# Hybrid decoder layer, one core: gate and up of the two FFNs with tokens stationary in blocks of 512 columns each, two of eight feature pairs by Strassen's products

## The chip, the cores and the metric

The kernel runs on one core of a Trainium2 chip. The metric is the device time of one execution in microseconds, lower is better. TensorE is called PE here, VectorE DVE, ScalarE ACT, GpSimd POOL, and SyncE SP (it issues the loads).

## The reference, cut to what matters

One layer for 256 tokens with 2048 features, in float32: an FFN, a mixing stage with two attentions, and a second FFN.

```python
def swiglu(x, w_gate, w_up, w_down):
    return (jax.nn.silu(x @ w_gate) * (x @ w_up)) @ w_down
...
f = swiglu(rmsnorm(x, ffn1_pre_g[l]), ffn1_w_gate[l], ffn1_w_up[l], ffn1_w_down[l])
x = x + FFN_RES_SCALE * rmsnorm(f, ffn1_post_g[l])
h = rmsnorm(x, mix_pre_g[l])
...
x = x + rmsnorm(o @ w_out[l], mix_post_g[l])
f = swiglu(rmsnorm(x, ffn2_pre_g[l]), ffn2_w_gate[l], ffn2_w_up[l], ffn2_w_down[l])
x = x + FFN_RES_SCALE * rmsnorm(f, ffn2_post_g[l])
```

Each FFN has 5632 hidden features: `w_gate` and `w_up` are 2048 x 5632, `w_down` is 5632 x 2048. A feature tile is 128 features, so the inputs have 16 tiles (8 pairs) and the hidden layer has 44 (22 pairs). A token tile is 128 tokens; there are two, t=0 and t=1.

## The kernel before

**Float32 in two halves.** Every operand of a large product is split into a high part `hi` and a rest `lo`, and a product is made of hi·hi, hi·lo and lo·hi. The class `Weights` loads weights in float32 into one of three buffers (`raw`, 1 MB each), SP issuing the loads in a fixed order. It then splits them into parts of up to 1024 columns: ACT casts the high part (`whi`, L133), DVE subtracts it from the original to give the rest (`wlo`, L138). There are four buffers for parts, and `get` asks for parts three ahead of the one that PE takes. So the cast of a part waits until PE has finished with the part four before it.

**Gate and up.** `gate_up(fp)` makes 256 gate features and 256 up features (the number `fp` runs from 0 to 21). Weights are stationary, x is the moving operand: for each input tile and each of two output tiles there is one product of `whi` with [hi x, lo x] side by side, 512 columns (L493), and one of `wlo` with hi x, 256 columns (L502). A part holds four input tiles, so it is 8 products of each kind. x itself is not yet scaled by the token's norm; the results are, by a row `pre.R` (L735, L743). The output has features on the partitions, as the down product needs it as its stationary operand; `put_h` splits it, and for the pairs that go by Strassen's products forms their sums first (`sum_h`).

**Down.** The class `Down` (L804) works with tokens stationary: h is the stationary operand and the weights move, 512 columns at a time. A pair of feature tiles times two chunks of 512 columns is a 2 x 2 block product. Plain, it takes 24 products into four accumulators, called 2, 3, 4 and X. By Strassen's scheme in Winograd's form (`BY_SUMS`, 4 of 11 pairs) it takes 7 block products, 21 in all, into seven accumulators 1 to 7; DVE forms the sums of the weights in place in the raw buffer (`add_sums`, L101 to L107), which makes a pair four parts instead of two. PSUM has eight banks of 512 columns. `middle` joins the seven accumulators, `finish` adds the last four.

**Order.** The hidden layer is done in two halves of 11 pairs: gate and up of a half, then its down products for two column ranges `u`. Steps of other engines are queued by `later(n, ...)` and taken up, one entry a part, by `step()`. Inside the handovers from one stage to the next (`handover`, `take_over`, `start`) the order is written out by hand; elsewhere a scheduler orders each engine's instructions and hands out PSUM banks and the 28 SBUF slots as they come free. POOL is used in the handovers and in the rotary part of one attention. The residual x stays in SBUF (`xn`) all the time.

## Time and profile before

| | |
|---|---|
| median of 3 runs | 1886.82 us (1886.21 to 1886.95) |
| the profiled execution | 1886.46 us, of which span 1884.4 us |
| granted PE clock, mean | 0.994 |
| busy | PE 98%, DVE 71%, ACT 51%, POOL 5% of the span |
| DMA | 188 GB/s, the core's engines 55% busy with the weights |

The span runs from the first to the last instruction; 2.06 us lie around it. Busy shares are averages over the stages. A matmul's own duration contains its latency, so what it costs is read from the spacing of starts, not from its duration.

### The profile page before, as it was taken

The numbers are of one execution on the slowest core, as the hardware profiler recorded it, in microseconds if no ns is written. First come the engines' busy times: TensorE is split into PE (matmuls) and PEld (weight loads), VectorE is DVE, ScalarE is ACT, GpSimd is POOL, SyncE is SP. The second block draws the span as 40 slices with busy tenths as digits, with TensorE's granted clock in tenths as the row PEclk, the third lists the DMA queues.
The fourth block names the chain that finished last, engine by engine and source line by source line (L and its number), as shares of the span: only waits on it lengthen the run. The fifth ranks groups of instructions, "written<-read, shape, count | busy, mean of one in ns | idle before, by whom it ended". The sixth has DMA issues, their size and how long they took to land.

```text
span 1884.4 us, 25317 instructions
## 1 busy us (share of the span) xinstructions
PE 1853.7 (98%) x9802; PEld 1595.8 (85%) x9802; DVE 1342.1 (71%) x1998; ACT 965.5 (51%) x1411; POOL 103.0 (5%) x92
## 2 busy tenths in 40 slices
PE   9999999999999998999999999999999999999997
PEld 8888888888888887788888887888888888888885
DVE  6666688766666998666786557766678766666897
ACT  6444455544444555645545446544455544444553
POOL 0000000000000002000352103000000000000001
PEclk9999999999999999999999999999999999999998
DMA  8555555665655554554445555555555665555453
GB/s 270 179 196 184 190 190 201 223 201 180 197 183 191 191 194 161 184 186 161 157 157 183 181 172 172 186 194 187 187 192 202 223 200 180 194 187 187 172 200 134
DMA packets 260120, 353.73 MB, mean 188 GB/s; under 512 B 5856, under 2 KB 219040, under 8 KB 259616
## 3 DMA queue, kind: packets, MB, share of 16 engines
q1 hardware_dynamic: 259552, 351.30, 55.1%
q8 instruction: 77, 1.26, 0.3%
q0 software_dynamic: 272, 0.75, 0.1%
q14 instruction: 43, 0.35, 0.1%
q10 hardware_dynamic: 176, 0.07, 0.0%
HBM read 350.00 MB, written 2.10 MB: 187 GB/s over the span
## 4 chain that ended last, share of the span: by engine, by line
PE 94%; DVE 4%; ACT 1%; issue 1%; POOL 0%; DMA 0%; DVEq 0%; ACTq 0%; POOLq 0%
PE p L493 34%; PE d L822 20%; PE p L502 18%; PE pq L493 5%; PE pw L512 4%; PE pv L512 4%; PE d_X L822 4%; PE pq L502 3%; DVE wlo L138 1%; DVE xn L673 1%; PE po L1020 0%; PE xt_f L456 0%; ACT sqd L365 0%; PE p L497 0%; ACT whi L133 0%
## 5 line engine op out<-in xcount | busy, mean ns | idle before, releaser
L138 DVE TENSOR_TENSOR wlo<-raw,whi 128x1024 fp32r<-128x1024 f32 (+1 forms) x717 | 859.3, 1209 | 487.5 <-ACT whi L133 482.3
L133 ACT CAST whi<-raw 128x1024 fp32r<-128x1024 f32 (+1 forms) x721 | 736.9, 1030 | 768.5 <-PE p L493 374.7
L493 PE MATMUL p<-xg_f,whi 128*128 128x512 f32 x2784 | 698.9, 392 | 0.0
L493 PEld LDWEIGHTS p<-xg_f,whi 128*128 128x128 f32 x2784 | 500.4, 189 | 89.2
L502 PEld LDWEIGHTS p<-xg_f,wlo 128*128 128x128 f32 x2816 | 384.8, 190 | 27.7
L502 PE MATMUL p<-xg_f,wlo 128*128 128x256 f32 x2816 | 394.0, 282 | 0.0
L822 PE MATMUL d<-whi,h 128*128 128x512 f32 x672 | 207.5, 389 | 0.0
L822 PEld LDWEIGHTS d<-whi,h 128*128 128x128 f32 x672 | 126.1, 188 | 26.2
L493 PE MATMUL pq<-xg_mix,whi 128*128 128x512 f32 x512 | 131.8, 399 | 0.0
L822 PE MATMUL d<-wlo,h 128*128 128x512 f32 x336 | 114.7, 390 | 0.0
L493 PEld LDWEIGHTS pq<-xg_mix,whi 128*128 128x128 f32 x512 | 92.2, 189 | 16.9
L512 PE MATMUL pv<-whi,xg_mix 128*128 128x512 f32 x256 | 85.4, 405 | 1.7 <-ACT xg_mix L422 1.7
L822 PE MATMUL d_X<-whi,h 128*128 128x512 f32 x224 | 85.5, 389 | 0.0
L652 ACT COPY right<-p 128x256 f32<-128x256 f32 x176 | 60.1, 370 | 45.5 <-PE p L493 40.9
L512 PE MATMUL pw<-whi,om 128*128 128x512 f32 x256 | 75.2, 391 | 0.0
L822 PEld LDWEIGHTS d<-wlo,h 128*128 128x128 f32 x336 | 62.9, 188 | 13.6 <-DVE wlo L138 0.6
L502 PEld LDWEIGHTS pq<-xg_mix,wlo 128*128 128x128 f32 x512 | 69.8, 190 | 5.3
L822 PE MATMUL d<-whi,hi 128*128 128x512 f32 x224 | 72.2, 390 | 1.3 <-ACT whi L133 1.3
L822 PE MATMUL d<-wlo,hi 128*128 128x512 f32 x224 | 71.8, 390 | 0.0
L822 PE MATMUL d<-whi,ho 128*128 128x512 f32 x224 | 71.6, 389 | 0.0
L502 PE MATMUL pq<-xg_mix,wlo 128*128 128x256 f32 x512 | 71.3, 282 | 0.0
L138 POOL TENSOR_TENSOR wlo<-raw,whi 128x512 fp32r<-128x512 f32 (+1 forms) x10 | 17.8, 1786 | 824.2 <-DVE rs_post_f L349 729.7
(198 smaller groups left out, 1486.5 us busy)
## 6 DMA issues: line engine op xcount, KB each, us to landing
raw<-in_ffn_w_down_dram SPq DMA_DIRECT2D x86, 1024.0 KB, 5.0
raw<-in_ffn_w_gate_dram SPq DMA_DIRECT2D x84, 1024.0 KB, 5.0
raw<-in_ffn_w_up_dram SPq DMA_DIRECT2D x84, 1024.0 KB, 5.0
raw<-in_w_in_dram SPq DMA_DIRECT2D x48, 1024.0 KB, 5.2
raw<-in_w_out_dram SPq DMA_DIRECT2D x16, 1024.0 KB, 4.9
raw<-in_ffn_w_up_dram SPq DMA_DIRECT2D x8, 512.0 KB, 3.5
raw<-in_ffn_w_gate_dram SPq DMA_DIRECT2D x7, 512.0 KB, 3.8
xn<-in_x_dram SPq DMA_DIRECT2D x8, 256.0 KB, 6.0
```

Of the source, the lines that this page charges most:

```text
L133: self.nc.scalar.copy(hi, raw)
L138: eng.tensor_sub(lo[:, k0:k1], raw[:, k0:k1], hi[:, k0:k1].bitcast(F32))
L493: nc.tensor.matmul(p, wh, x, start=k == 0, stop=False)
L502: nc.tensor.matmul(p[:, :T], lo[:, j, f * P:(f + 1) * P], xs(k)[:, 0, :], start=False, stop=k == KD - 1)
L512: nc.tensor.matmul(ps[c], y, w[:, j, c * CH:(c + 1) * CH], start=first and n == 0, stop=last and n == 2)
L652: nc.scalar.copy(t, ps[:, T:])
L673: nc.vector.scalar_tensor_tensor(x, f, self.z[t], x, op0=ALU.mult, op1=ALU.add)
L822: nc.tensor.matmul(self.ps[x], y, w, start=m == 1, stop=m == self.n[x])
```

## The change

Only `fp` 0 and 1 of each FFN (the first 256 + 256 features each time, which stand in the handover) are still made the old way. From then on, gate and up are made in ten blocks of 512 gate and 512 up columns (`gate_up_block`) by a class `Block` that is the old `Down` made general: x is the stationary operand, the weights move, the two chunks of a 2 x 2 block product are 512 gate and 512 up columns, and two of the eight pairs of input tiles (`X_SUMS`, pairs 1 and 4) go by Strassen's products. Five blocks belong to the first half of the hidden layer, which now has 12 pairs, and five to the second, which has 10; the down products are by sums for 4 pairs of the first half and 3 of the second.

Since the results now have tokens on the partitions, x must be scaled before the products (`scale_x`, on ACT, in place in `xn`), turned and split once more (`put_x`, 32 PE transposes in each FFN, in the last three steps of `fp` 1), and the product h of each block must be turned back into features on partitions (`turn_h`, 8 transposes a block, after the first pair of the next block or of the down product). Accumulators of gate and up are joined, passed through silu and multiplied in `xn`, which serves as scratch. So the residual is kept in DRAM: in FFN 1 it is read again from the input, in FFN 2 it is written out after the handover; both times POOL issues eight loads of 256 KB during the second half's down products. The loads of gate and up become two of 512 KB for each pair instead of one of 1 MB. Gains of rows and the attention's masks move to SBUF slots, of which there are 30 now.

```diff
-BY_SUMS = (0, 2, 4, 6)
-KP = KF // 4
+X_SUMS = (1, 4)
+
+
+FIRST, BLOCKS = 1, (6, 11)
+HALVES = (
+    ((0, 2, 1, 4, 3, 6, 5, 8, 7, 9, 10, 11), (2, 4, 6, 8), ()),
+    ((13, 12, 15, 14, 17, 16, 18), (12, 14, 16), (19, 20, 21)),
+)
+H_SUMS = HALVES[0][1] + HALVES[1][1]
...
-    slots = Slots(ctx.enter_context(tc.tile_pool(name="slots", bufs=1)), 28)
+    slots = Slots(ctx.enter_context(tc.tile_pool(name="slots", bufs=1)), 30)
...
-        for fp in range(KF // 2):
+        for fp in range(2 * FIRST):
...
+        for half in range(2):
+            for u in range(BLOCKS[half - 1] if half else FIRST, BLOCKS[half]):
+                plan["block", n, u] = [
+                    (q, W.add_sums((wg, wu), 2 * q, u * CH) if q in X_SUMS else W.add((wg, wu), 2 * q, 2, u * CH, 2 * CH))
+                    for q in range(KD // 2)
+                ]
+            plan_down(n, half, wd)
...
+                for c in range(NC):
+                    for t in range(NT):
+                        sl = slice(c * CH, (c + 1) * CH)
+                        nc.gpsimd.dma_start(kept[:, t, sl], xn[:, t, sl])
...
+        def sums_of(r, name):
+
+            a21 = r[:, 7]
+            nc.vector.tensor_add(r[:, S1], a21, r[:, A22])
+            nc.vector.tensor_sub(r[:, S3], r[:, A11], a21)
+            nc.vector.tensor_sub(r[:, S2], r[:, S1], r[:, A11])
+            nc.vector.tensor_sub(r[:, S4], r[:, A12], r[:, S2])
+            hi, lo = (slots.take([P, 7, P], F32R, f"{name}{m}") for m in "hl")
+            nc.scalar.copy(hi, r[:, :7])
+            nc.vector.tensor_sub(lo, r[:, :7], hi.bitcast(F32))
+            return hi, lo
...
+        def scale_x(c):
+            for t in range(NT):
+                x = xn[:, t, c * CH:(c + 1) * CH]
+                nc.scalar.activation(x, x, AF.Copy, scale=pre.z[t])
+
+        def put_x(q):
+            ps = bank(f"xt{n}{q}")
+            for j in range(2):
+                for t in range(NT):
+                    m = 2 * j + t
+                    k = 2 * q + j
+                    nc.tensor.transpose(ps[:, m * P:(m + 1) * P], xn[:, t, k * P:(k + 1) * P], ident)
+            name = f"x{n}_{q}"
+            gains = [pre.gains[:, 2 * q + j:2 * q + j + 1] for j in range(2)]
+            if q in X_SUMS:
+                r = slots.take([P, 8, P], F32, f"r{name}")
+                p4 = ps.rearrange("p (m c) -> p m c", c=P)
+                nc.scalar.activation(r[:, 0::7], p4[:, :2], AF.Copy, scale=gains[0])
+                nc.scalar.activation(r[:, 1:3], p4[:, 2:], AF.Copy, scale=gains[1])
+                xx[q] = sums_of(r, name)
+                slots.give(f"r{name}")
+            else:
+                xx[q] = slots.take([P, 2, 2, T], F32R, name)
+                for j in range(2):
+                    for f in split_rows(xx[q][:, j], ps[:, j * T:(j + 1) * T], gains[j]):
+                        f()
...
+                banks(0), banks(1)
+                for c in range(NC):
+                    later(c, lambda c=c: scale_x(c))
+                if n == 1:
+                    later(5, lambda: turn_gains(G, graw, G_END))
+                for q in range(KD // 2):
+                    later(5 + q // 3, lambda q=q: put_x(q))
...
-        class Down:
-
-
-            def __init__(self, half, u):
-                self.half, self.c = half, (2 * u, 2 * u + 1)
+        class Block:
+
+
+            def __init__(self, name, pairs, xs, sums, more=0):
+                self.name, self.pairs, self.xs, self.sums = name, pairs, xs, sums
                 self.ps, self.done = {}, {}
-                self.pairs = plan["down", n, half, u]
-                sums = len(BY_SUMS)
-                self.n = {x: 3 * sums for x in "1234567"}
-                self.n["X"] = 0
-                for x in "234X":
-                    self.n[x] += 6 * (KP - sums)
...
+                by_sums = len([p for p, _ in pairs if p in sums])
+                plain = len(pairs) + more - by_sums
+                self.n = {x: 3 * by_sums * (x != "X") + 6 * plain * (x in "234X") for x in "1234567X"}
...
+
+                def first():
+                    nc.scalar.copy(a, self.ps["1"])
+                    nc.vector.tensor_add(b, self.ps["6"], a)
+                    nc.vector.tensor_sub(c, b, self.ps["5"])
+
+                def second():
+                    nc.vector.tensor_add(d, self.ps["7"], c)
+                    nc.vector.tensor_add(b, self.ps["7"], b)
...
+        def gate_up_block(u):
+
+            tg = [xn[:, 0, m * CH:(m + 1) * CH] for m in range(NC)]
+            blk = Block(f"b{n}{u}", plan["block", n, u], xx, X_SUMS)
+            blk.run(waiting, blk.joins(*(tg[m] for m in (0, 2, 1, 3))), lambda p: None)
+            for c, t in ((1, 0), (0, 0), (0, 1), (1, 1)):
+                blk.join(tg[2 * t + c], c, t)
+            for t in range(NT):
+                g, h = tg[2 * t], tg[2 * t + 1]
+                nc.scalar.activation(g, g, AF.Silu)
+                later(t, lambda g=g, h=h: nc.vector.tensor_mul(h, h, g))
+            waiting.append(lambda: turn_h(u, tg))
+
+        def turn_h(u, tg):
+
+            for m in range(2):
+                p = 2 * u + m
+                name = f"h{n}_{p}"
+                ps = bank(f"ht{n}{p}")
+                p4 = ps.rearrange("p (m c) -> p m c", c=P)
+                for j in range(2):
+                    for t in range(NT):
+                        k = 2 * m + j
+                        nc.tensor.transpose(p4[:, 2 * j + t], tg[2 * t + 1][:, k * P:(k + 1) * P], ident)
+                if p in H_SUMS:
+                    r = xn[:, 1, m * 8 * P:(m + 1) * 8 * P].rearrange("p (m c) -> p m c", c=P)
+                    nc.scalar.copy(r[:, 0::7], p4[:, :2])
+                    nc.scalar.copy(r[:, 1:3], p4[:, 2:])
+                    later(m, lambda p=p, r=r, name=name: hx.__setitem__(p, sums_of(r, name)))
+                else:
+                    hx[p] = slots.take([P, 2, 2, T], F32R, name)
+                    v = ps.rearrange("p (j t) -> p j t", j=2)
+                    nc.scalar.copy(hx[p][:, :, 0], v)
+                    nc.vector.tensor_sub(hx[p][:, :, 1], v, hx[p][:, :, 0].bitcast(F32))
...
+        if n == 1:
+            kept = xv
+        else:
+            kept = tc.dram_tile([P, NT, D], F32, name="kept")
+        for fp in range(2 * FIRST):
+            gate_up(fp)
+        slots.give(*pre.names)
         for half in range(2):
-            for fp in range(half * KP, (half + 1) * KP):
-                gate_up(fp)
+            for u in range(BLOCKS[half - 1] if half else FIRST, BLOCKS[half]):
+                gate_up_block(u)
             if half == 0:
-                post = Post(f"f{n}", row_gain(row_name), half=True)
+                post = Post(f"f{n}", half=True)
             else:
-                slots.give(*pre.names)
+                for q, x in xx.items():
+                    give(x, f"x{n}_{q}")
                 more = [slots.take([P, 2, CH], F32, f"more{n}{m}") for m in range(2)]
+                post.rows = RowGain(row_name)
+                for c in range(NC):
+                    for t in range(NT):
+                        sl = slice(c * CH, (c + 1) * CH)
+                        later(8 + c, lambda t=t, sl=sl: nc.gpsimd.dma_start(xn[:, t, sl], kept[:, t, sl]))
             for u in range(2):
                 d = Down(half, u)
-                d.run()
+                d.go()
                 if (half, u) != (1, 1):
                     for c, t in ((1, 0), (0, 0), (0, 1), (1, 1)):
                         d.finish(c, t)
         d.tail(end_of(post))
-        slots.give(*(f"more{n}{m}" for m in range(2)), *(f"h{n}_{KF // 2 - 3 + m}" for m in range(3)))```

What moves on the engines, at three places. **First, PE in gate and up.** Before, a part looks like this (`p_2_0` and `p_2_1` are the accumulators of two gate tiles, `xg_f` is x turned, `whi` and `wlo` are a part of the weights; of each kind there are eight rows in turn):

```order
L493 MATMUL p_2_0_781<-xg_f_102,whi_725 128x512
L493 MATMUL p_2_1_782<-xg_f_102,whi_725 128x512
...
L493 MATMUL p_2_0_781<-xg_f_103,whi_725 128x512
...
L502 MATMUL p_2_0_781<-xg_f_102,wlo_726 128x256
L502 MATMUL p_2_1_782<-xg_f_102,wlo_726 128x256
...
L502 MATMUL p_2_0_781<-xg_f_103,wlo_726 128x256
```

Now, at the end of a block's first pair (`x_0`) and in its second (`x_1h`, `x_1l`, by sums), with `b_1` to `b_7` and `b_X` the accumulators and `ht` the banks in which the block before is turned:

```order
L872 MATMUL b_4_1471<-whi_1411,x_0_646 128x512
L872 MATMUL b_X<-whi_1411,x_0_646 128x512
L952 MATMUL ht_1497<-ident,xn 128x128
L952 MATMUL ht_1504<-ident,xn 128x128
L872 MATMUL b_1_1519<-whi_1430,x_1h 128x512
...
L872 MATMUL b_2_1463<-whi_1454,x_1l 128x512
L952 MATMUL ht_1497<-ident,xn 128x128 x3
L952 MATMUL ht_1504<-ident,xn 128x128 x3
L872 MATMUL b_5_1545<-whi_1480,x_1h 128x512
...
L872 MATMUL b_7_1547<-whi_1480,x_1h 128x512
...
L872 MATMUL b_6_1558<-whi_1512,x_1h 128x512
```

All products are 512 wide, and eight transposes of the block before stand between them in two groups, the second group after nine products of the second pair; `b_7` and `b_6` come last, in the banks of `ht`.

**Second, DVE between two blocks.** Before, from one `fp` to the next, DVE had splits with steps of 256 columns between them:

```order
L138 TENSOR_TENSOR wlo_848<-raw_829,whi_847 128x1024
L138 TENSOR_TENSOR wlo_870<-raw_829,whi_869 128x1024
L654 TENSOR_TENSOR u<-p_2_0_781,right 128x256
L654 TENSOR_TENSOR g<-p_2_1_667,right 128x256
L743 TENSOR_TENSOR u<-u,R_f_480 128x256
L735 TENSOR_TENSOR g<-g,R_f_480 128x256
L716 TENSOR_TENSOR hr_2_922<-u,g 128x2x128
```

Now the last joins of a block (L924), the sums of the next block's second pair (L104 to L110), its splits (L142) and the product of gate and up (L939, once for each token tile) follow each other:

```order
L142 TENSOR_TENSOR wlo_1431<-raw_1415,whi_1430 128x1024
L924 TENSOR_TENSOR xn<-b_3_1123,xn 128x512
L104 TENSOR_TENSOR raw_1415<-raw_1415 128x512
...
L924 TENSOR_TENSOR xn<-b_4_1129,xn 128x512
L924 TENSOR_TENSOR xn<-b_X,xn 128x512
L142 TENSOR_TENSOR wlo_1455<-raw_1415,whi_1454 128x512
L109 TENSOR_TENSOR raw_1415<-raw_1415 128x512
L939 TENSOR_TENSOR xn<-xn 128x512
L110 TENSOR_TENSOR raw_1415<-raw_1415 128x512
L142 TENSOR_TENSOR wlo_1481<-raw_1415,whi_1480 128x1024
L939 TENSOR_TENSOR xn<-xn 128x512
L142 TENSOR_TENSOR wlo_1513<-raw_1415,whi_1512 128x1024
```

There are ten instructions from the first split to the first L939 (two of them, a join and a sum, are under the dots), and three more to the second; each group of transposes needs one of the L939.

**Third, PE in `fp` 1**, where nothing but products of the first kind stood before:

```order
L525 MATMUL p_1_1_448<-xg_f_103,wlo_515 128x256
L337 MATMUL gp<-ident,graw 128x48
L807 MATMUL xt_641<-ident,xn 128x128 x4
L807 MATMUL xt_651<-ident,xn 128x128 x4
L807 MATMUL xt_667<-ident,xn 128x128 x4
L516 MATMUL p_1_0_447<-xg_f_104,whi_547 128x512
...
L807 MATMUL xt_700<-ident,xn 128x128 x4
L807 MATMUL xt_710<-ident,xn 128x128 x4
L807 MATMUL xt_726<-ident,xn 128x128 x4
```

The transposes of `put_x` stand after each of the last three parts, three banks (`xt`), three and two.

## Rows read from the trace of the kernel before

**Rows 1.** The page: busy time of each engine, share, instructions.

```profile
PE 1853.7 (98%) x9802; PEld 1595.8 (85%) x9802; DVE 1342.1 (71%) x1998; ACT 965.5 (51%) x1411; POOL 103.0 (5%) x92
```

**Rows 2.** By stretch: gate and up, then down, of FFN 1's first half.

```profile
core 0: us, PE busy (x) PEld busy (x) DVE busy (x) ACT busy (x) POOL busy (x), PEclk, DMA share, GB/s
41.00:258.00 217.00, 217.00 (x1241) 190.76 (x1240) 144.12 (x217) 105.24 (x154) 0.00 (x0) 1.00 0.58 191
258.00:373.00 115.00, 115.00 (x512) 95.36 (x511) 95.22 (x109) 60.96 (x66) 0.00 (x0) 1.00 0.58 205
```

**Rows 3.** What PE waited for: us in total, times, longest; the largest.

```profile
PE xt_f L456 <- DVE xn L673: 3.7, 4, 2.7
```

**Rows 4.** The critical chain: start, us, what; 39 parts lie between them.

```profile
63.60 1.84 PE p L493 x8
...
172.54 1.84 PE p L493 x8
```

**Rows 5.** Timeline of PE in a down product: start, us, line, operands, count.

```profile
289.60 0.62 PE L822 MATMUL d<-whi,hi 128*128 128x512 f32 x2
...
294.36 0.62 PE L822 MATMUL d<-whi,h 128*128 128x512 f32 x2
...
307.96 0.62 PE L822 MATMUL d<-whi,h 128*128 128x512 f32 x2
```

**Rows 6.** Groups of PE by form: count, then busy us and mean ns.

```profile
L493 PE MATMUL p<-xg_f,whi 128*128 128x512 f32 x2784 | 698.9, 392 | 0.0
L502 PE MATMUL p<-xg_f,wlo 128*128 128x256 f32 x2816 | 394.0, 282 | 0.0
```

**Rows 7.** Timeline of PE around eight transposes in FFN 1's handover.

```profile
19.39 1.04 PE L456 MATMUL xt_f<-ident,xn 128*128 128x128 f32 x8
20.19 1.63 PE L493 MATMUL p<-xg_f,whi 128*128 128x512 f32 x6
```

**Rows 8.** The tile `xt_f`: durations in ns, least, median, greatest.

```profile
L456 PE MATMUL xt_f<-ident,xn x64: 270/273/474, 5.8 to 1163.7; 128*128 128x128 f32 x64
```

**Rows 9.** Timeline of DVE in a down product, where it runs without a pause.

```profile
298.37 1.22 DVE L138 TENSOR_TENSOR wlo<-raw,whi 128x1024 fp32r<-128x1024 f32 x1
299.51 1.28 DVE L867 TENSOR_TENSOR fg_f<-d,fg_f 128x512 f32<-128x512 f32 x2
...
311.84 0.68 DVE L138 TENSOR_TENSOR wlo<-raw,whi 128x512 fp32r<-128x512 f32 x1
312.44 0.69 DVE L106 TENSOR_TENSOR raw<-raw 128x512 f32<-128x512 f32 x1
...
315.87 1.88 DVE L874 TENSOR_TENSOR fg_f<-d,fg_f 128x512 f32<-128x512 f32 x3
317.67 0.68 DVE L874 TENSOR_TENSOR fg_f<-d_X,fg_f 128x512 f32<-128x512 f32 x1
```

**Rows 10.** Timeline of ACT in the same down product.

```profile
291.42 2.95 ACT L133 CAST whi<-raw 128x1024 fp32r<-128x1024 f32 x3
...
300.00 1.05 ACT L133 CAST whi<-raw 128x1024 fp32r<-128x1024 f32 x1 [1.67 <-PE d_X L822]
```

**Rows 11.** Groups of DVE and ACT by form: count, busy us, mean ns.

```profile
L138 DVE TENSOR_TENSOR wlo<-raw,whi 128x1024 fp32r<-128x1024 f32 x677 | 828.2, 1232 | 487.5 <-ACT whi L133 482.3 <-ACT right L652 1.9
...
L728 DVE TENSOR_TENSOR ho<-hr,hi 128x896 fp32r<-128x896 f32 x16 | 17.4, 1085 | 1.2 <-ACT hi L727 1.2
...
L423 DVE SCALAR_TENSOR_TENSOR xg_f<-xt_f,G,xg_f 128x256 fp32r<-128x256 f32 x20 | 8.3, 476 | 4.7 <-ACT xg_f L422 4.7
...
L722 DVE TENSOR_TENSOR hr<-hr 128x128 f32<-128x128 f32 x16 | 4.7, 292 | 0.5
...
L652 ACT COPY right<-p 128x256 f32<-128x256 f32 x176 | 60.1, 370 | 45.5 <-PE p L493 40.9 <-DVE g L654 3.4 <-DVE u L654 1.3
```

**Rows 12.** A load (KB, median us to landing), and POOL's time to issue one.

```profile
raw<-in_ffn_w_up_dram SPq DMA_DIRECT2D x8, 512.0 KB, 3.5
...
L994 POOL DMA_DIRECT2D mixc<-mconsts_dram x1 | 0.6, 604 | 0.8 <-DVE xg_mix L423 0.8
```

## What the change does to the time, predicted

> **What bounds the kernel now.** I read the page first: PE is busy 98% of the span, DVE 71%, ACT 51%, POOL 5% [rows 1]. Then the stretches, because a share of the whole hides what one stage does: in gate and up and in the down products of FFN 1 PE is busy for every microsecond at clock 1.00, with DVE at 66% (144 of 217) and 83% (95 of 115) beside it [rows 2]. PE's own waits lie in the handovers, the largest sum being 3.7 us [rows 3]. So in the stages that the change touches the time is the sum of PE's spacings, and nothing else gives or takes anything until it makes PE wait. Less work on PE is worth its full price, and each new wait of PE costs its full length.
>
> **What PE loses and gains.** An old part (8 products of 512 columns, 8 of 256) has its start repeated every 2.793 us (108.94 us for 39 parts) [rows 4]. A 512-column product in the form that the blocks take over, x or h stationary and weights moving, is spaced 226.7 ns, by sums (4.76 us for 21) as well as plain (13.60 us for 60) [rows 5]. There were 2784 and 2816 of the old products [rows 6], and in the changed program's order 224 and 256 of them stay, so 2560 of each go, 320 parts: 320 x 2.793 = 893.9 us. Each of the 20 blocks has 6 plain pairs of 24 products and 2 by sums of 21, which is 186; 3720 x 0.2267 = 843.2 us. The down products have 7 pairs by sums instead of 8 over both halves, so 3 products more for each column range, 12 in all, 2.7 us. Net 893.9 - 843.2 - 2.7 = **47.9 us less**. Of the 2.5 us a block, 1.2 do not come from Strassen: 24 products for a plain pair take 5.44 us where two old parts took 5.59, eight times over. The rest is 3 products saved twice.
>
> Against this stand the transposes: 8 x 20 for h and 32 x 2 for x, 224. Eight of them in the first handover take 0.80 us from their first start to the next product [rows 7], 100 ns each, so **22.4 us more**. The duration of one is 273 ns [rows 8], but the next starts long before it ends. The Trainium skill ("TensorE: Matmul & The Clock Gate", Part 4: PE-mode transpose) gives about 275 ns for a transpose in a kernel's context and speaks of latency; taken as a price it would make the 224 cost 61.6 us, by my estimate, and turn the net into a loss of about 14 us. The trace agrees with that figure as a duration and not as a spacing. I go by the spacing; the bounds of the price are 100 and 273 ns.
>
> So PE's own work falls by 25.5 us. What remains is whether DVE and ACT keep up.
>
> **The waits between two blocks.** For a block DVE has 18 splits of 1024 columns and 2 of 512, 8 sums, 8 joins, 2 products and the turned h. Back to back, DVE's instructions start 1.14 us apart for 1024 columns and 0.60 for 512 (298.37 to 299.51; 311.84 to 312.44; three joins in 1.80) [rows 9]; their durations are about 0.08 longer [rows 11]. That is 20.5 + 1.2 + 4.8 + 4.8 + 1.2 + 2.5 = 35.0 us of the block's 43.0: enough room in the mean, but it is uneven. Let 0 be the moment at which PE begins a block. ACT can cast the first part of the second pair only when PE gives up the part four before it, and does so 0.2 us after the next part's start (the release at 300.00) [rows 10], that is at -2.5; DVE subtracts it from -1.4. From there DVE has no pause: that split, four joins, two sums, the half split, a third sum and the first product are 1.14 + 9 x 0.60 = 6.5, ready at 5.2. PE wants the first two transposes after 24 products, at 5.44: no wait. Then a sum, a split and the second product, 2.3 more: ready at 7.55. PE is there after 2 transposes and 9 products, 7.68: no wait. Then PE wants two banks in which h was turned. ACT copies them out after the casts of two parts that PE gave up at 7.2 and 7.9: casts until 9.1 (three start to start take 0.95 each [rows 10]), two copies of 0.37 [rows 11], free at 9.85 where PE wants it at 9.64: 0.2 us of waiting. The second bank is freed by DVE at 11.0 and wanted at 11.2. After that DVE is ahead again and the second pair by sums (pair 4) finds its parts ready, its weights too: their buffer is free at about 8.6, two loads of 512 KB take 3.5 us each or more [rows 12], and PE needs them at 22.
>
> So every margin is 0.1 to 0.2 us. If all instructions took their whole durations, the 16 or so in that chain would come 16 x 0.08 = 1.3 us later and PE would wait for nearly all of it. The bounds are 0 and 1.3 us a block; the spacing was seen in just such a stream, so I take a value near it, 0.4, **8 us more** in 20 blocks (0 to 26). If DVE is late here, what is late next is the transposes, and behind them in PE's queue the whole second pair.
>
> **Setting up x.** From the first group of x's transposes PE has 3.2 us of transposes, two old parts (5.6), the first pair (5.4) and 9 products (2.0) before it needs the third part of the second pair: 16.3 us. DVE must by then make 12 splits of x (0.48 by duration, 0.42 spaced), sums and splits for two pairs (8 at 0.22, 2 at 1.0) [rows 11], 4 weight splits, 4 sums and what is left of `fp` 0 and 1: 5.0 + 3.8 + 4.0 + 2.4 + 1.4 = 16.6, beginning 1.3 late for the same reason as above, and a bank more has to be freed behind it. PE waits some 2 us, twice 2.5 with what ACT adds: **5 us more** (0 to 10).
>
> **The residual.** POOL issues 8 stores and twice 8 loads at 0.6 us each [rows 12]. The stores stand between its splits in FFN 2's handover, where it is mostly idle; I take 1 us (0 to 5). The loads come in the second half's down products, where PE has no wait for a load worth a row and the DMA engines are busy 58% [rows 2]; 2 MB beside some 20 MB are hidden. Nothing, with 3 us as the bound. `scale_x` is 8 passes of 512 columns on ACT, which is busy half of the time [rows 2]; if that cover were gone, 8 times half a cast, 8 x 0.5 = 4 us [rows 10]. It is part of the bound of 10 above.
>
> **Sum**, against the profiled execution's own 1886.5: -47.9 + 22.4 + 8 + 5 + 1 = -11.5, so **1875**. The median of the runs is 0.4 above that execution, which changes nothing.
>
> **Rivals.** *No waits*: DVE keeps every margin and the set-up is hidden: 1886.5 - 25.5 = 1861. For it speaks that PE waited for nothing where DVE stood at 83% [rows 2]; against it, that here the burst at the block's start is DVE's at 100% for 11 us. *DVE's chain decides, slower*: each block's first transposes wait. At 1.3 us a block the time is 1861 + 26 + 6 = 1893. It passes into slower from 1.2 us a block, (1890.6 - 1867) / 20. For it speak the full durations and that all four places hang on one engine; against it, the spacings. *In between*: 0.8 to 1.2 us a block, 1883 to 1890, no change that can be told. *A transpose costs its duration*, because the groups of two and six stand between products of another kind: 1875 + 224 x 0.173 = 1914. The eight in the handover stood between such products too, so little speaks for it. The Trainium skill's figure named above would lead here. *The change does not do what it says*, in that the blocks' products are not spaced 227 ns because parts come late all the time: DVE's 35.0 of 43.0 us speaks against that; it would show as a block longer than 45 us, the old 16 parts being 44.7.
>
> **Chances and range.** Forecast (1864 to 1883) 0.61; no waits (1858 to 1864) 0.14; in between 0.10; DVE's chain slower 0.11; transposes at their duration 0.03; blocks late throughout 0.01. A measurement of this kernel can tell about 0.2%, 3.8 us, from no change. Faster 0.75, same 0.10, slower 0.15. The range, 1860 to 1890, takes in the forecast, most of the first rival and the case in between, and leaves out just under 0.2; the forecast's own range is 1864 to 1883.
>
> **What would show it.** In the profile after, the block's products stand 226.7 ns apart and a block repeats every 43.0 to 43.9 us. Transposes come eight to 0.8 us. DVE's busy time rises by some 106 us, to 77% of the span: 20 blocks of 35.0 where two old `fp` took 44.7 x 0.66 = 29.7 [rows 2]. PE's waits name DVE or ACT at the `ht` transposes and at the banks 6 and 7, in sum 0 to 15 us, and some 5 us around `xt` and the first block. It is wrong if a block takes 45 us, if PE waits over 1 us at each `ht`, if transposes are spaced over 150 ns, or if loads appear among PE's or ACT's long waits.

## The result, and the profile after

The changed kernel takes 1872.98 us (median of 4, 1872.38 to 1873.18) against 1886.51 (1885.75 to 1886.95): ratio 0.9928, 95% interval 0.9911 to 0.9945, so 13.5 us faster, more than the 3.8 us that a measurement can tell. 1875 was predicted, range 1860 to 1890. The page's busy times after, as in [rows 1]:

```profile
PE 1837.3 (98%) x8638; PEld 1530.4 (82%) x8638; DVE 1480.8 (79%) x2026; ACT 1012.3 (54%) x1359; POOL 115.4 (6%) x117
```

PE is still busy 98%, with 1164 instructions fewer (1388 products fewer, 224 transposes more); DVE rose by 139 us. The same stretches of time as [rows 2]; the second now begins with the last 20 us of gate and up, down runs from 278.0:

```profile
core 0: us, PE busy (x) PEld busy (x) DVE busy (x) ACT busy (x) POOL busy (x), PEclk, DMA share, GB/s
41.00:258.00 217.00, 216.66 (x1005) 179.12 (x1005) 183.74 (x246) 124.01 (x162) 1.13 (x2) 1.00 0.55 189
258.00:373.00 115.00, 115.00 (x512) 95.18 (x512) 96.37 (x108) 61.54 (x67) 0.00 (x0) 1.00 0.54 197
```

In gate and up DVE went from 144 to 184 of 217 us, PE's clock stays at 1.00. What PE, and its weight loads (PEld), waited for (us in total, times, longest):

```profile
PE xt_f L479 <- DVE xn L696: 3.5, 3, 2.7
...
PEld b L872 <- ACT xn L956: 5.2, 14, 0.4
...
PEld d L872 <- ACT whi L137: 3.3, 4, 1.0
PEld b L872 <- DVE wlo L142: 2.4, 3, 0.8
```

The first answers [rows 3]. New are the waits at a bank (the second row: `b`, until ACT has copied the turned h, L956) and for weights in the first block of each FFN (the fourth). A row of PEld tells how long the weight loads stood still; part of that lies behind products still running, so what PE loses is read below from its starts. The timeline of PE where a block begins (start, us, line, operands, count), and the same place one block earlier as first line:

```profile
110.08 0.38 PE L952 MATMUL ht<-ident,xn 128*128 128x128 f32 x2
...
153.43 0.38 PE L952 MATMUL ht<-ident,xn 128*128 128x128 f32 x2
153.56 0.71 PE L872 MATMUL b<-whi,x_1h 128*128 128x512 f32 x2
154.11 0.62 PE L872 MATMUL b<-wlo,x_1h 128*128 128x512 f32 x2
...
155.71 0.82 PE L952 MATMUL ht<-ident,xn 128*128 128x128 f32 x6
156.28 0.48 PE L872 MATMUL b<-whi,x_1h 128*128 128x512 f32 x1
156.59 0.40 PE L872 MATMUL b<-wlo,x_1h 128*128 128x512 f32 x1
...
157.52 0.40 PE L872 MATMUL b<-whi,x_1l 128*128 128x512 f32 x1
157.86 0.50 PE L872 MATMUL b<-whi,x_1h 128*128 128x512 f32 x1
158.19 0.39 PE L872 MATMUL b<-wlo,x_1h 128*128 128x512 f32 x1
```

A block repeats every 43.35 us (153.43 - 110.08). Its 186 products at 226.7 ns are 42.17. Two transposes take 0.13, six 0.57, and the product behind each group is followed late, by 0.10 (0.55 for two) and 0.08 (0.31 for one): 0.88 for eight, 0.11 each. From 157.52 two spacings take 0.67 in place of 0.45: 0.22 us is the wait at the bank of the seventh product. That makes 43.27 of 43.35. The durations of the transposes, which answer to [rows 8]:

```profile
L952 PE MATMUL ht<-ident,xn x160: 270/272/273, 110.1 to 1758.6; 128*128 128x128 f32 x160
```

### The profile page after: what moved, and what is told of

Its sections match the earlier page's. It is cut to its first block, busy times and chain, and to the rows that moved or that the text cites. A ratio compares the mean times of both kernels' runs of the same rounds, so it can differ in the third digit from the quotient of the medians.

```text
span 1871.2 us, 23266 instructions
## 1 busy us (share of the span) xinstructions
PE 1837.3 (98%) x8638; PEld 1530.4 (82%) x8638; DVE 1480.8 (79%) x2026; ACT 1012.3 (54%) x1359; POOL 115.4 (6%) x117
## 4 chain that ended last, share of the span: by engine, by line
PE 91%; DVE 5%; ACT 1%; issue 1%; DMA 1%; POOL 0%; DVEq 0%; ACTq 0%; POOLq 0%
PE b L872 36%; PE d L872 19%; PE b_X L872 9%; PE pq L516 6%; PE pw L535 4%; PE pv L535 4%; PE d_X L872 4%; PE pq L525 3%; PE p L516 2%; DVE wlo L142 1%; PE p L525 1%; PE ht L952 1%; DVE xn L696 1%; ACT whi L137 1%; DMA raw<-in_ffn_w_gate_dram 0%
## 5 line engine op out<-in xcount | busy, mean ns | idle before, releaser
L137 ACT CAST whi<-raw 128x1024 fp32r<-128x1024 f32 (+1 forms) x793 | 790.9, 1014 | 735.4 <-PE b_X L872 301.0
L142 DVE TENSOR_TENSOR wlo<-raw,whi 128x1024 fp32r<-128x1024 f32 (+1 forms) x789 | 919.6, 1186 | 335.6 <-ACT whi L137 333.2
L872 PE MATMUL b<-whi,x 128*128 128x512 f32 x1440 | 443.9, 389 | 0.0
L872 PEld LDWEIGHTS b<-whi,x 128*128 128x128 f32 x1440 | 270.2, 188 | 56.3
L872 PE MATMUL b<-wlo,x 128*128 128x512 f32 x720 | 243.9, 389 | 0.7 <-DVE wlo L142 0.7
L872 PE MATMUL d<-whi,h 128*128 128x512 f32 x720 | 222.6, 389 | 0.4 <-ACT whi L137 0.4
L872 PE MATMUL b_X<-whi,x 128*128 128x512 f32 x480 | 186.9, 389 | 0.0
L872 PEld LDWEIGHTS b<-wlo,x 128*128 128x128 f32 x720 | 135.0, 188 | 29.6 <-DVE wlo L142 1.6
L872 PEld LDWEIGHTS d<-whi,h 128*128 128x128 f32 x720 | 135.0, 188 | 29.3 <-ACT whi L137 1.3
L516 PE MATMUL pq<-xg_mix,whi 128*128 128x512 f32 x512 | 131.8, 399 | 0.0
L872 PE MATMUL d<-wlo,h 128*128 128x512 f32 x360 | 122.5, 389 | 0.0
L516 PEld LDWEIGHTS pq<-xg_mix,whi 128*128 128x128 f32 x512 | 92.2, 189 | 16.9
L872 PEld LDWEIGHTS b_X<-whi,x 128*128 128x128 f32 x480 | 90.1, 188 | 19.0 <-issue 0.4
L872 PE MATMUL b_X<-wlo,x 128*128 128x512 f32 x240 | 93.4, 389 | 0.0
L872 PE MATMUL d_X<-whi,h 128*128 128x512 f32 x240 | 91.8, 389 | 0.0
L872 PEld LDWEIGHTS d<-wlo,h 128*128 128x128 f32 x360 | 67.6, 188 | 14.1
L525 PEld LDWEIGHTS pq<-xg_mix,wlo 128*128 128x128 f32 x512 | 69.8, 190 | 5.3
L525 PE MATMUL pq<-xg_mix,wlo 128*128 128x256 f32 x512 | 71.3, 282 | 0.0
L516 PE MATMUL p<-xg_f,whi 128*128 128x512 f32 x224 | 58.1, 397 | 0.0
## 6 DMA issues: line engine op xcount, KB each, us to landing
raw<-in_ffn_w_up_dram SPq DMA_DIRECT2D x168, 512.0 KB, 4.8
raw<-in_ffn_w_gate_dram SPq DMA_DIRECT2D x167, 512.0 KB, 3.8
```

What stands on the lines that cost most here:

```text
L137: self.nc.scalar.copy(hi, raw)
L142: eng.tensor_sub(lo[:, k0:k1], raw[:, k0:k1], hi[:, k0:k1].bitcast(F32))
L516: nc.tensor.matmul(p, wh, x, start=k == 0, stop=False)
L525: nc.tensor.matmul(p[:, :T], lo[:, j, f * P:(f + 1) * P], xs(k)[:, 0, :], start=False, stop=k == KD - 1)
L872: nc.tensor.matmul(self.ps[x], y, w, start=m == 1, stop=m == self.n[x])
```

## The experiments

My theory: PE's spacing is the price of everything as long as DVE, in its order, delivers each block's parts. The rivals: the form alone gains, transposes cost their duration, the waits come of something else than the bank, and VectorE's load is the bound. Every kernel was timed beside the kernel before, whose median was 1886.0 to 1886.3.

**Without Strassen's products in gate and up.**

```diff
-X_SUMS = (1, 4)
+X_SUMS = ()
```

(The joins become copies.)

> No pair of feature tiles of gate and up is taken by Strassen's products: the form with tokens stationary alone, its transposes and its x set-up stay. Theory (TensorE's spacing is the price of everything): 2 pairs x 20 blocks x 3 products = 120 products come back at 226.7 ns = +27.2 us; the wait at the bank of the seventh product (about 0.215 us in 16 blocks, 3.4 us) and up to 2.8 us of waits around the two first blocks go. 1873.0 + 27.2 - 3.4 to 6.2 = 1894 to 1897, that is slower than the kernel before by 8 to 10 us. Rival A (the form pays, fewer and longer products, and Strassen's products only add waits and VectorE work): 1868 to 1876. Rival B (VectorE, freed of the sums, gives back half of it elsewhere): 1882 to 1888.

1894.29 us (1893.57 to 1895.46), ratio 1.0043 (1.0030 to 1.0055). The form alone is a loss of 8.0 us, and rivals A and B fall. By the prediction's own terms it should be -893.9 + 3840 x 0.2267 + 2.7 + 22.4 + 6 = +7.7. The 6 are the prediction's 5 for setting up x and 1 for the residual, which this kernel's rows do not show; without them, and with 0.11 for a transpose, it is +3.9. So the close match is partly luck. 1.4 of the 4.1 us missing are waits at the transposes (`ht` <- DVE xn, 2.9 us in 16 in PEld's rows): the scheduler has put the second group of six one product behind the first two, in place of nine.

**Each transpose of h twice.**

```diff
-                for j in range(2):
+                for j in [*range(2), *range(2)]:
```

> Each of the eight transposes of h that a block issues is issued twice, one behind the other into the same place: 160 more transposes, nothing else. Theory (in a stream a transpose costs its spacing, 109 ns by the starts of the changed kernel, not its duration of 272 ns): 160 x 0.109 = +17.4 us, 1890.4 (1888 to 1892). Rival A (each costs its duration): 160 x 0.272 = +43.5 us, 1916.5. Rival B (they lie in time in which TensorE would wait for h or for a bank anyway): 1873 to 1877.

1892.72 us (1891.86 to 1894.44), 19.7 more than the changed kernel. The timeline of PE in that kernel:

```profile
1250.87 0.38 PE L952 MATMUL ht<-ident,xn 128*128 128x128 f32 x2
...
1253.17 1.69 PE L952 MATMUL ht<-ident,xn 128*128 128x128 f32 x14
1254.62 0.47 PE L872 MATMUL b<-whi,x_1h 128*128 128x512 f32 x1
...
1295.19 0.38 PE L952 MATMUL ht<-ident,xn 128*128 128x128 f32 x2
```

Fourteen take 1.45 us to the next product where six took 0.57: 0.88 for eight more, 17.6 us in 20 blocks. The rest is a longer wait behind them (the block repeats every 44.32, 0.97 more). A price by duration would have been 43.5 us and is 24 us off. The Trainium skill ("TensorE: Matmul & The Clock Gate", Part 4: PE-mode transpose) gives about 275 ns for a transpose in one kernel's context, in a sentence on bf16. The trace has that figure, in float32, as the duration (272), and this run measures what a further one costs in a stream: 0.11.

**The pairs by sums one place later.**

```diff
-X_SUMS = (1, 4)
+X_SUMS = (2, 5)
```

> The two pairs by Strassen's products are the third and the sixth of a block in place of the second and the fifth; the same work. Theory (the wait at the bank of the seventh product comes of the first pair by products beginning 5.4 us behind the last joins, and 24 more plain products, 5.4 us, cover it; the first block's waits for weights by sums get the same time): -3.4 us from 16 blocks and up to -2.8 us from the two first blocks, 1867 to 1870. Rival A (the time between products there is a property of the products by sums and no wait for a bank): 1873. Rival B (the joins, one pair later, push the chain joins, silu, product, transposes past its margin of 0.1 to 0.2 us): 1875 to 1885.

1867.55 us (1866.78 to 1867.95), 5.4 less than the changed kernel; the rows `b <- ACT xn` and `b <- DVE wlo` are gone from its waits. 14 blocks at 0.22 make 3.1, and in the two first blocks PE's starts were late by 2.9: 6.0. So these waits were the bank's and the weights'. The joins a pair later cost little: `ht` <- DVE xn is a new row, 2.9 us in 16, of which PE loses 1.4 by its starts. The scheduler moved the second group of transposes here too (two at 108.34, six at 108.83, one product between), so the bank is free sooner as well as wanted later, and the two are not parted. The kernel without sums has the same order and the same row at `ht`, so the comparison with it is clean: 26.74 us for 120 products, 223 ns each (0.2267 x 120 = 27.2).

**The residual's transfers left out** (stores L774, loads L1038).

```diff
-                        nc.gpsimd.dma_start(kept[:, t, sl], xn[:, t, sl])
+                        pass
...
-                        later(8 + c, lambda t=t, sl=sl: nc.gpsimd.dma_start(xn[:, t, sl], kept[:, t, sl]))
+                        pass
```

> The changed kernel without the transfers of the residual: neither stored to DRAM in the first FFN nor loaded back behind the blocks in either; so what is added as the residual is not x (that part of the computation is changed). Theory (the stores and reloads lie beside TensorE's products, and the add waits for nothing): 1872 to 1874. Rival A (the loads, issued by GpSimd while weights come, delay weights by 0.3 to 0.5 us a tile): 1868 to 1871. Rival B (the handover's first add waits for its reload): 1869 to 1870.

1872.59 us (1871.89 to 1873.06) against 1872.38 to 1873.18: nothing that can be told. (The stores are those of FFN 2's handover, 1134 to 1153 us of the changed kernel, not of the first FFN as the expectation has it; FFN 1 reads its input again.)

**One more VectorE instruction ahead of each product of gate and up.**

```diff
-                later(t, lambda g=g, h=h: nc.vector.tensor_mul(h, h, g))
+                later(t, lambda g=g, h=h: (nc.vector.tensor_copy(g, g), nc.vector.tensor_mul(h, h, g)))
```

> The changed kernel with one more VectorE instruction of about 0.6 us (a copy of silu's result onto itself) ahead of each of a block's two products of gate and up; the result is the same. Theory (the chain joins, silu, product, transposes has 0.2 to 0.25 us of room: the two products end at 109.83 and 112.17, the transposes that need them start at 110.08 and 112.39): the first two transposes come 0.35 to 0.4 us late, the other six 1.0 in all, 20 blocks x 0.9 to 1.1 = +18 to 22 us, 1889 to 1895. Rival A (the order hides it, as VectorE is idle for 17% of a block): 1873 to 1876. Rival B (only the first delay counts, since the second product runs while TensorE is late already): 1879 to 1882.

1877.94 us (1877.58 to 1879.15), 5.0 more, so none of the three as written. The program's order on PE has moved:

```diff
-L952 MATMUL ht_1155<-ident,xn 128x128
-L952 MATMUL ht_1162<-ident,xn 128x128
-L872 MATMUL b_1_1177<-whi_1088,x_1h 128x512
 L872 MATMUL b_3_1123<-whi_1088,x_1h 128x512
-L872 MATMUL b_1_1177<-wlo_1089,x_1h 128x512
 L872 MATMUL b_3_1123<-wlo_1089,x_1h 128x512
-L872 MATMUL b_1_1177<-whi_1088,x_1l 128x512
 L872 MATMUL b_3_1123<-whi_1088,x_1l 128x512
 L872 MATMUL b_2_1121<-whi_1112,x_1h 128x512
+L952 MATMUL ht_1157<-ident,xn 128x128
+L952 MATMUL ht_1164<-ident,xn 128x128
```

The first two transposes now stand behind four products that need no h. The scheduler that writes the order saw the longer chain and gave PE other work, so this run changed two things and does not measure the room of 0.1 to 0.2 us. The copy was also shorter than I took it for (0.34 us from start to start). By the starts of PE, 3.1 of the 5.0 us lie in down and 1.3 in the blocks, and the rows that grew are waits for casts: `d <- ACT whi` from 3.3 to 7.4 and `b <- ACT whi` from 0.6 to 4.4. At the transposes there is still no row.

**Three pairs by sums.** For the room in SBUF one pair of down goes back to plain products.

```diff
-X_SUMS = (1, 4)
+X_SUMS = (2, 4, 6)
...
-    ((0, 2, 1, 4, 3, 6, 5, 8, 7, 9, 10, 11), (2, 4, 6, 8), ()),
+    ((0, 2, 1, 4, 3, 6, 5, 8, 7, 9, 10, 11), (2, 4, 6), ()),
```

> Three pairs of a block by Strassen's products (the third, fifth and seventh) in place of two; for the room that this takes one pair of the first half of down goes back to plain products (4 pairs by products become 3). Theory (TensorE's spacing decides as long as VectorE has room in a block): 60 gate and up products fewer, 12 down products more, -48 x 0.2267 = -10.9 us, and the bank's wait goes as in the kernel with the sums one pair later, -3.4: 1858 to 1863. VectorE gets 4 sums of 0.6 us and loses one split of about 0.6 us of low parts in a block: 36.1 + 1.8 = 37.9 of 42.7 us, 89%. Rival (VectorE in order is already late at 83%, so each further pair costs waits for weights by sums of 0.5 us a block or more): 1868 to 1880.

1861.48 us (1860.19 to 1864.71). Inside the blocks PE has one wait with a row, 0.5 us in the first block of FFN 2, with VectorE busy 120.67 of 127 us in three others. 4.8 of the 10.9 us expected against the two pairs at (2, 5) are missing (1867.55 - 1861.48 = 6.1), and 4.4 of them stand in down by PE's starts. The two largest of the rows that grew (3.2 and 1.0 with the pairs at (2, 5)):

```profile
PEld d L872 <- ACT whi L137: 5.3, 8, 1.0
...
PEld d L872 <- DVE wlo L142: 4.1, 11, 0.6
```

**Three pairs, and both halves of down in another order.**

```diff
-    ((0, 2, 1, 4, 3, 6, 5, 8, 7, 9, 10, 11), (2, 4, 6), ()),
-    ((13, 12, 15, 14, 17, 16, 18), (12, 14, 16), (19, 20, 21)),
+    ((0, 1, 2, 3, 5, 4, 7, 6, 8, 9, 10, 11), (2, 4, 6), ()),
+    ((13, 15, 12, 14, 17, 16, 18), (12, 14, 16), (19, 20, 21)),
```

> Three pairs of a block by Strassen's products as before, and in down the first pair by products is third in place of second, in both halves (0, 1, 2, 3, 5, 4, ... and 13, 15, 12, 14, ...). Theory (the waits of 0.25 to 0.8 us at the start of each down block are for weights by sums that stand in VectorE's order behind the joins of the block before; with three pairs they sum to about 6 us): 2 to 5 us go, 1856 to 1860. Rival (the waits come of the first weights of down whatever pair they belong to, or of VectorE being full to the end of the last block): 1860 to 1863.

1861.48 us (1860.61 to 1862.09), no gain. In the first half both rows are gone. In the second 12 and 14 now stand side by side, and the row for `whi`, all of it there, grew to 7.3:

```profile
PEld d L872 <- ACT whi L137: 7.3, 8, 1.2
```

**Three pairs, and the second half of down alone spread.**

```diff
-    ((13, 12, 15, 14, 17, 16, 18), (12, 14, 16), (19, 20, 21)),
+    ((13, 15, 12, 17, 14, 18, 16), (12, 14, 16), (19, 20, 21)),
```

> Three pairs as in the kernel that took 1861.5 us, the first half of down as there, the second half in the order 13, 15, 12, 17, 14, 18, 16: a plain pair stands between any two by products, and two ahead of the first (in the kernel that changed both halves 12 and 14 stood side by side, and the waits came at 14). Theory (the waits at the start of the second half's blocks are for weights by sums in VectorE's order, and another plain pair covers them): 2 to 4 us go, 1857.5 to 1860. Rival (they move to the next pair by sums again): 1861 to 1863.

**1856.57 us** (1855.54 to 1856.81), ratio 0.9841 (0.9827 to 0.9854): 16.4 us faster than the changed kernel and the fastest here. Of the row for `whi` 1.0 is left, of the other 1.6, all in the first half of down, whose order is as before; in the second half both are gone. From two pairs at (2, 5) it is 11.0 us, where 48 products make 10.9; the new order of down takes away waits that the two pairs had too, so the match is partly luck.

**Four pairs.** Two pairs of down go back to plain products.

```diff
-X_SUMS = (1, 4)
+X_SUMS = (2, 3, 5, 6)
...
-    ((0, 2, 1, 4, 3, 6, 5, 8, 7, 9, 10, 11), (2, 4, 6, 8), ()),
+    ((0, 2, 1, 4, 3, 6, 5, 8, 7, 9, 10, 11), (2, 4), ()),
```

> Four pairs of a block by Strassen's products (the third, fourth, sixth and seventh); two pairs of the first half of down go back to plain products for the room. Theory (VectorE has its limit in the block: it was busy 36.1 us a block in the changed kernel and 40.3 with three pairs, so 4.2 a pair, and a fourth makes 44.5, against 42.4 - 3 x 0.227 = 41.7 us that TensorE needs): TensorE waits for weights by sums, a block takes 43.5 to 44.5 us, 20 blocks + 22 to + 42 us on the 1861.5 of three pairs, less what is caught up on in down: 1875 to 1900. Rival (TensorE's spacing alone, VectorE never the bound): 96 products fewer than the changed kernel and the banks' wait gone, 1873.0 - 21.8 - 5 = 1846 to 1851.

1946.47 us (1944.24 to 1947.39). Slower as expected, but by far more than the 1875 to 1900 that the load of VectorE gave. A part is PE's clock (last section). Its waits stand at the second of two adjacent pairs, hence the next kernel; in this one place and load are not parted.

**Three pairs, two of them adjacent** (down as in the kernel of 1856.57).

```diff
-X_SUMS = (2, 4, 6)
+X_SUMS = (2, 3, 6)
```

> The kernel that took 1856.6 us (three pairs, the second half of down with plain pairs between) with the three pairs of a block at the third, fourth and seventh place in place of the third, fifth and seventh: the same work for every engine, two pairs by products side by side. Theory (what held up the kernel with four pairs is above all the place: its waits stand at the second pair of each two side by side, 0.9 to 1.0 us at each of two parts; two such pairs want 4.2 + 2.4 us of VectorE's work each within 9.5 us of TensorE, and only four parts are made ahead): 1.5 to 2.5 us a block, 20 blocks, 1886 to 1907. Rival (the load of a whole block decides, 40.3 of 42.4 us, wherever the pairs stand): 1855 to 1860.

1899.47 us (1896.23 to 1902.28): 42.9 more than the same work with a plain pair between, and the transposes stand alike in both (two, six products, six). The place decides. PE, then DVE, then ACT in one block of it (in brackets the idle time before, and what ended it):

```profile
199.24 0.38 PE L952 MATMUL ht<-ident,xn 128*128 128x128 f32 x2
...
211.95 0.39 PE L872 MATMUL b<-whi,x_3l 128*128 128x512 f32 x1
213.21 0.73 PE L872 MATMUL b<-whi,x_3h 128*128 128x512 f32 x2 [0.87 <-ACT whi L137]
214.67 0.50 PE L872 MATMUL b<-whi,x_3h 128*128 128x512 f32 x1 [0.72 <-ACT whi L137]
...
243.82 0.38 PE L952 MATMUL ht<-ident,xn 128*128 128x128 f32 x2
```

```profile
210.59 0.69 DVE L104 TENSOR_TENSOR raw<-raw 128x512 f32<-128x512 f32 x1
211.31 0.69 DVE L105 TENSOR_TENSOR raw<-raw 128x512 f32<-128x512 f32 x1
212.04 0.69 DVE L109 TENSOR_TENSOR raw<-raw 128x512 f32<-128x512 f32 x1
212.76 0.69 DVE L110 TENSOR_TENSOR raw<-raw 128x512 f32<-128x512 f32 x1
```

```profile
212.11 1.05 ACT L137 CAST whi<-raw 128x1024 fp32r<-128x1024 f32 x1 [3.12 <-DVE raw L105]
213.57 4.84 ACT L137 CAST whi<-raw 128x1024 fp32r<-128x1024 f32 x5 [0.41 <-DVE raw L110]
```

DVE forms the second pair's sums from 210.59 on, ACT's cast of them starts when they are there, and PE, which began that pair at 210.14, waits for that cast: the third and fourth part of the pair have nothing made ahead. From 211.95 to 213.21 one spacing takes 1.26 us in place of 0.23, and from 213.21 to 214.67 two take 1.46 in place of 0.45: 2.0 us. A block repeats every 44.58 us (243.82 - 199.24); with the pairs spread it was 42.41.

**Two of four sums on GpSimd.**

```diff
-            eng.tensor_add(q[:, 3], q[:, 3], q[:, 0])
-            eng.tensor_sub(q[:, 2], q[:, 2], q[:, 3])
+            pool = self.nc.gpsimd if isinstance(w, tuple) else eng
+            pool.tensor_add(q[:, 3], q[:, 3], q[:, 0])
+            pool.tensor_sub(q[:, 2], q[:, 2], q[:, 3])
```

> Four pairs by Strassen's products, as in the kernel that took 1946.5 us, with two of the four sums that each pair of gate and up needs of its weights on GpSimd in place of VectorE. Theory (that kernel's blocks of 46.5 us are VectorE's: its 44 us of work a block, and the steps at which ScalarE and VectorE wait for each other, one sum behind the other): VectorE loses 4 x 2 x 0.6 = 4.8 us a block, GpSimd's row of a 128x512 subtraction is 1.65 to 1.8 us and lies beside; the blocks come back to 42 to 43.5 us, 1851 to 1880. Rival A (the chain from sum to rounding to low parts decides, not VectorE's load; GpSimd's sums of 1.7 us make it longer): 1940 to 1970. Rival B (TensorE alone again): 1848.

> Three pairs by Strassen's products as in the kernel that took 1861.5 us, with the same two sums a pair on GpSimd. VectorE's busy time in a block falls from 40.3 to about 36.7 of 42.4 us. Theory (with three pairs TensorE's spacing decides inside the blocks; VectorE at 95% only costs the 3 to 6 us of waits where the blocks end and down begins): 1856 to 1860. Rival (GpSimd's sums are longer and come late for the weights' next split): 1863 to 1880.

2059.53 us (2057.53 to 2063.34) with four pairs, 1926.23 (1925.12 to 1927.19) with three. VectorE's load fell (by 75 and 48 us, from 83% to 75 and 78% of the spans) and the time rose by 113 and 65 us against the same kernels with all sums on VectorE. So less load did not help; the cause may be the longer chain from sum to cast to low part, or the hold-up between GpSimd and VectorE shown at the end, which these two runs do not part. With four pairs the clock has a share: by the mean granted clocks (0.967 against 0.985) I estimate up to 40 of the 113 us; with three it has none (0.994 against 0.993). In the kernel with three pairs (durations in ns, least, median, greatest):

```profile
L110 POOL TENSOR_TENSOR raw<-raw x60: 1291/1297/2291, 69.6 to 1787.8; 128x512 f32<-128x512 f32 x60
L111 POOL TENSOR_TENSOR raw<-raw x60: 1299/2152/2309, 72.0 to 1789.2; 128x512 f32<-128x512 f32 x60
```

In each pair's chain 1.3 + 2.2 us stand where VectorE needed 1.2.

## Why the prediction was right, point by point

**PE's spacing is the time**: right. PE stays at 98%, and 120 products more or fewer moved the time by 223 ns each.

**-47.9 for the products**: right. In the changed kernel the products of a block stand 226.7 ns apart, and the kernels without sums and with sums later differ by 26.7 us where 27.2 were due.

**+22.4 for the transposes**: the mechanism was right, the size a little low. 0.11 each with the product behind them, 24.6 for 224, not 100 ns. x's 64 cost the same in the changed kernel's trace:

```profile
56.67 1.47 PE L807 MATMUL xt<-ident,xn 128*128 128x128 f32 x12
57.90 2.09 PE L516 MATMUL p<-xg_f,whi 128*128 128x512 f32 x8
```

Twelve take 1.23 to the next product; FFN 1's 32 take 3.31, and the product behind each group is followed 0.09 late.

**+8 for the waits between blocks**: mis-sized. It measured 0.22 us in 14 blocks, 3.1 us, and all of it at one of the four places, the seventh product's bank, at which I had worked out 0.2 and then taken 0.4. (Two more blocks follow a block whose turned pairs both go by plain products; they have no copy L956 and no wait.) No wait at the `ht` transposes is in the rows. My fear that full durations would eat the margins was unfounded in this order; how much room the chain has was not measured, since the scheduler moved the transposes when I lengthened it.

**+5 for setting up x**: little over half the size. In the first blocks PE's starts are late by 0.6 us in FFN 1 and 2.3 in FFN 2, nearly all in front of weights (PEld's rows: 2.4 for low parts, 0.6 for casts). In FFN 2 they begin at the third part of the second pair, which is the place named, in FFN 1 in the pair behind it; x's own transposes and splits have no row among PE's waits.

**+1 for the residual, loads hidden**: right within what can be told (0.4 us, intervals overlapping).

**Signs**: DVE rose by 139 us, not 106 (a block takes 36.1 us, 108.3 busy of 130 us in three blocks, not 35.0; that is 22 of the 33 us missed, and the rest, probably x's set-up, was not in that sum). The block is 43.35 us, inside 43.0 to 43.9.

**The sum**: with the measured terms it is -47.9 + 24.6 + 3.1 + 2.9 + 0 = -17.3 against -13.5. The starts of PE place most of the 3.8 us between: down's products wait for weights 1.2 longer (3.4 us of late starts, 2.2 before), a block is 0.08 longer than the parts listed above (1.6 in 20), and 0.7 lies where both kernels run the same code (the first transposes start 0.3 later, the mixing stage takes 0.4 more). None of these was in the prediction's sum. So the mechanism was right, and that the forecast came within 2 us is partly luck: the waits, the set-up and the residual were put 8.0 us too high, the transposes 2.2 too low, and 3.8 us were missing.

The rival of VectorE's chain did not come: no wait at `ht` in this kernel. What did cost 43 us in another kernel, two pairs by sums side by side, is a different chain of VectorE's, from sums to casts, which the prediction did not name.

## What to carry to other kernels

On an engine that is full, price an instruction by its spacing in a stream of its kind, and a new form of the work by all that it adds: here the form lost 8 us and only 120 saved products made it a gain. When operands are made by a chain of two other engines, spread the pairs that need the long chain: with VectorE at 95% of the blocks and three pairs spread PE hardly waited, and with the same work and two pairs side by side it waited 2 us a block. And after an edit look at the order that the scheduler wrote before calling it a test of one thing: here it moved the transposes of h in kernels whose edits did not touch them.

## What the runs showed of the hardware

The clock: in the kernel with four pairs PE waited 0.87 and 0.72 us, and then this (windows, us; columns as in the first section):

```profile
218.00:220.20 2.20, 1.27 (x4) 0.78 (x5) 2.15 (x3) 1.79 (x3) 0.00 (x0) 1.00 0.16 61
220.20:223.60 3.40, 3.40 (x9) 2.62 (x8) 3.40 (x4) 2.35 (x3) 0.00 (x0) 0.50 0.45 107
```

For 3.4 us the granted clock was 0.50, 1.2 GHz, and products started 0.43 us apart (two from 220.64 to 221.50 in its timeline) in place of 0.227: a wait was paid about twice. From the mean granted clocks (0.985, and 0.994 in the changed kernel) I estimate some 58 us at 0.50 in that kernel and some 22 in the changed one. In the kernel with two adjacent pairs the same two waits left it at 1.00 (214.60 to 219.00).

GpSimd and VectorE hold each other up. While GpSimd formed sums (the first two rows) VectorE's 128x128 sums took this (the other three), in the kernel with three pairs:

```profile
207.49 1.29 POOL L110 TENSOR_TENSOR raw<-raw 128x512 f32<-128x512 f32 x1 [19.05 <-DVE raw L105]
208.86 1.42 POOL L111 TENSOR_TENSOR raw<-raw 128x512 f32<-128x512 f32 x1
207.97 0.96 DVE L782 TENSOR_TENSOR xn<-xn 128x128 f32<-128x128 f32 x1
208.85 0.28 DVE L783 TENSOR_TENSOR xn<-xn 128x128 f32<-128x128 f32 x1
209.06 1.37 DVE L784 TENSOR_TENSOR xn<-xn 128x128 f32<-128x128 f32 x1
```

0.96 and 1.37 us where 0.28 is usual, and each ended 0.15 us behind the GpSimd instruction beside it (208.78 and 210.28). The Trainium skill ("Trainium Architecture — The Big Picture", What this means for kernel authors) calls the port that the two share an exclusive lock, not a split of bandwidth; the trace agrees for these instructions.
